# Keeping four engines in written order through the projection of a transformer block, and loading the second half's x later

## Chip, cores and metric

The kernel runs on one core of a Trainium2 chip. The metric is the time of one execution on the device in microseconds (us); the time given for a kernel is the median of several executions.

## What is computed

The reference is one layer of a decoder trunk over 2048 positions of 1024 channels. Cut to what matters here:

```python
h = rms_norm(x, g_mix) * (1.0 + sc1) + sh1      # sh1, sc1 from silu(c) @ w_ada + b_ada
p = h @ w_in                                    # one combined projection, N_IN columns
q_a, k_a, v_a, q_m, k_m, v_m, o_m, u_s, v_s, f_a, i_m, f_m = split(p)
y_attn  = forgetting_attention(rms_norm(q_a), rms_norm(k_a), v_a, f_a)
y_mlstm = sigmoid(o_m) * rms_norm(mlstm_chunkwise(q_m, k_m, v_m, i_m, f_m))
y_sgu   = spatial_gating(gelu(u_s), gelu(v_s), ...)
x = x + gt1 * (concat([y_attn, y_mlstm, y_sgu]) @ w_out)
x = x + gt2 * conv_ffn(rms_norm(x) * (1.0 + sc2) + sh2)
```

Everything that the change touches lies in the first two lines, in the mLSTM and spatial gating groups, and in the start of the attention.

## The kernel before, in words

**The projection.** It takes the first 760 us or so of the execution. The sequence is cut into two halves of 1024 positions, the columns of `w_in` into seven blocks: KM with the gates, QO (queries and output gate of the mLSTM), VM, US (spatial gating), K, Q and V. The 14 steps are the seven blocks for the first half and then QO, KM, VM, US, K, Q and V for the second; "K of the second half" and so on names one of them. A step has eight results, each a tile `acc` in PSUM that 24 matmuls fill: eight parts of the contraction, and for each the three products of a split float32 (`mm3`, L54 to L56, with `wh` and `wl` as the high and low part of the weights and `hh`, `hl` of h).

**The lanes.** The other work is written as generators, called lanes (L459). The function `slot` (L462) is called after each result, and in blocks of 512 columns also after the fourth part of a result, so that half a result is the unit of delay; each call lets every lane that is due write its next piece. Lanes are: the rest of the modulation vectors (`rest_of_mod`), four quarters of the mLSTM (`mlstm(0)` to `mlstm(3)`, with a pace in slots), each closed by `mlstm_end` (L1020: H is divided, squared into `hq` by ScalarE L1032, summed on VectorE L1035, raised to a power on GpSimd L1037, scaled on VectorE L1039, transposed on TensorE L1045, multiplied with the gate `om` and stored in `yt_d`), the spatial gating (`spatial`, L754: two matmuls L761 in one PSUM tile, each read by VectorE L762), the norms and transposes of q and k (`use_qk`, L786: L789, L794, L795, L128, L799, L803, L807, L808, with the stores L810), and `refill`, which loads the eight x tiles of the second half, norms them and transposes them (L589) into h. Before the last step, V of the second half, all lanes are run out in a loop; then the attention's first loads (`kk` L157, `nf` L158, `q` L173, `vv` L163) and its first scores (L206) are written as one more lane beside V's matmuls.

**What sets the order.** Each engine has one queue of instructions. The Python code gives an order, but a scheduler reorders each engine's instructions by its own estimate before the program is built, so what stands in a queue need not be in written order. SyncE (SP) issues the DMAs, in its own queue, one after the other. Tiles of one tag share a number of buffers, and a new tile waits until the oldest has been read for the last time: the tag `t4k` has five buffers (L357) and holds x tiles, `om`, `hq` and the tiles of the spatial gating; raw weights `wr` have three, their split parts `wh` and `wl` eleven each.

**The first block.** KM of the first half is written by `first_block`. It computes part of the modulation on the way (`first_mod`: partial sums on VectorE and GpSimd, then matmuls L447), and norms and transposes the first eight x tiles (L542, L555, L589, L593 to L595).

Of the kernel before, what the change touches and what calls it, by code (L numbers as in the profile page):

```python
# [12 lines left out]
ALU = mybir.AluOpType  # L13
# [20 lines left out]
def trunk(  # L34
# [7 lines left out]
    V, A, G, T = nc.vector, nc.scalar, nc.gpsimd, nc.tensor  # L42
# [84 lines left out]
    def rsqrt(t, n):  # L127
        G.tensor_tensor(t, t, nhalf[:, 0:1].broadcast_to([P, n]) if n > 8 else nhalf[:, :n], op=ALU.pow)  # L128
# [246 lines left out]
    def misc_ps():  # L375
        return pp.tile([P, 512], F32, name="mp", tag="mp")
# [25 lines left out]
    def load_x(tt):  # L402
        xt = pool.tile([P, D], F32, name="xt", tag="t4k")
        dma(xt, x[tt * P : (tt + 1) * P, :])
        return xt
# [53 lines left out]
    def lane(steps_, delay=1, own=False):  # L459
        lanes.append([now[0] + delay, steps_, own])  # L460
# [59 lines left out]
    def small_setup():  # L520
        rows = []
        for i in range(2):
            r = pool.tile([P, P], F32, name="crow", tag="tmpA")
            if i == 0:
                dma(r[0:44], w_conv[0, 0].rearrange("(k p) -> k p", p=P))
                dma(r[44:88], w_conv[0, 1].rearrange("(k p) -> k p", p=P))
            else:
                dma(r[0:44], w_conv[0, 2].rearrange("(k p) -> k p", p=P))
                dma(r[44:88], b_conv[0].rearrange("(k p) -> k p", p=P))
            rows.append(r)  # L530
        yield 3
        for i, r in enumerate(rows):
            ps = misc_ps()
            T.transpose(ps[:, 0:88], r[0:88, :], ident[0:88, 0:88])
            V.tensor_copy(colC[:, i * 88 : (i + 1) * 88], ps[:, 0:88])
            yield 1

    def norm_sums(xt):
        st = pool.tile([P, 2], F32, name="st", tag="st")
        for q in range(2):  # L540
            jk = pool.tile([P, 512], F32, name="jk", tag="sq")
            A.activation(jk, xt[:, q * 512 : q * 512 + 512], AF.Square, accum_out=st[:, q : q + 1])  # L542
        V.tensor_tensor(st[:, 0:1], st[:, 0:1], st[:, 1:2], op=ALU.add)
        st = st[:, 0:1]
        V.tensor_scalar(st, st, 1.0 / D, EPS, op0=ALU.mult, op1=ALU.add)
        rsqrt(st, 1)
        return st
# [37 lines left out]
    def make_h(tb, xs, ks=range(KT)):  # L585
        for k in ks:
            ps = (tr_ps, misc_ps, tr_ps)[k % 3]() if tb == 0 else tr_ps()
            for i in range(4):
                T.transpose(ps[:, i * P : (i + 1) * P], xs[i][:, k * P : (k + 1) * P], ident)  # L589
            h32 = pool.tile([P, TB], F32, name="h32", tag="t2k")  # L590
            hh = pool.tile([P, TB], F32R, name="hh", tag="hT")
            hl = pool.tile([P, TB], F32R, name="hl", tag="hT")
            A.activation(h32, ps, AF.Identity, bias=sh1[:, k : k + 1], scale=a1[:, k : k + 1])  # L593
            V.tensor_copy(hh, h32)
            V.tensor_tensor(hl, h32, hh.bitcast(F32), op=ALU.subtract)  # L595
            hT[tb, k] = (hh, hl)
# [221 lines left out]
    def log_gates():  # L818

        fox, fm = gates[:, :, 64:72], gates[:, :, 32:36]  # L820
        mn = pool.tile([P, 8, 12], F32, name="lg0", tag="lg")
        ab = pool.tile([P, 8, 12], F32, name="lg1", tag="lg")
        for sl, g in ((slice(0, 8), fox), (slice(8, 12), fm)):
            V.tensor_scalar(mn[:, :, sl], g, 0.0, None, op0=ALU.min)
            V.scalar_tensor_tensor(ab[:, :, sl], mn[:, :, sl], 2.0, g, op0=ALU.mult, op1=ALU.subtract)
        A.activation(ab, ab, AF.Exp)
        A.activation(ab, ab, AF.Ln, bias=1.0)
        yield 1
        for sl, g in ((slice(0, 8), fox), (slice(8, 12), fm)):
            V.tensor_tensor(g, mn[:, :, sl], ab[:, :, sl], op=ALU.subtract)  # L830
# [189 lines left out]
    def mlstm_end(t0, H, ecol):  # L1020
# [21 lines left out]
        for j in range(2):  # L1042
# [5 lines left out]
            dma(yt_d[512 + j * P : 640 + j * P, t0 : t0 + 512], yt)  # L1048
            yield 1

    def refill():
        xs = [load_x(8 + t) for t in range(4)]
        yield 3
        for h in range(2):
            pair = xs[2 * h : 2 * h + 2]
            sts = [norm_sums(xt) for xt in pair]
            yield 1
            for xt, st in zip(pair, sts):
                V.tensor_scalar(xt, xt, st, None, op0=ALU.mult)
            yield 1  # L1060
        yield 1
        for k in range(KT):
            make_h(2, xs, (k,))
            if k not in (4, 6):
                yield 1
        xs = [load_x(12 + t) for t in range(4)]
        yield 4
        for h in range(2):
            pair = xs[2 * h : 2 * h + 2]
            sts = [norm_sums(xt) for xt in pair]  # L1070
            yield 1
            for xt, st in zip(pair, sts):
                V.tensor_scalar(xt, xt, st, None, op0=ALU.mult)
        yield 1
        for k in range(0, KT, 2):
            make_h(3, xs, (k, k + 1))
            yield 1
# [60 lines left out]
    def in_turn(*gens):  # L1138
        for g_ in gens:
            yield from g_  # L1140

    for n, (half, i) in enumerate(steps):
        if n == 1:
            lane(in_turn(log_gates(), iter((6,)), small_setup()), 2)
            lane(rest_of_mod(), 1)
        if n == 4:
            lane(in_turn(mlstm(0, 4), mlstm(1, 4)), 2)
        if n == nb - 1:
            lane(refill(), 1)
        if n == nb + 2:  # L1150
            lane(in_turn(log_gates(), iter((2,)), mlstm(2, 2), mlstm(3, 2)), 2)
        if n == len(steps) - 1:
            while any(not ln[2] for ln in lanes):
                slot()
            n_accs[0] = 2
            pool.close("proj_r")
            pp.close("proj_r")
            attention_open_right()

            load_k(0)  # L1160
            first_rows = [], []
            first = [scores(0, tb, load_q(0, tb, "qA"), r) for tb, r in zip((1, 0), first_rows)]
            load_v(0, (0, 1))
            lane(in_turn(*first), 1, True)
        light[0] = i < 3 or (half, i) == (0, 6)
        nxt[0] = Weights(blocks[steps[n + 1][1]][0]) if n + 1 < len(steps) else None
        if n == 0:
            first_block()
        else:
            blocks[i][1](half, cur)  # L1170
        if nxt[0]:
            nxt[0].cast()
        cur = nxt[0]
    pool.close("proj_l")
    pp.close("proj_l")

# [70 lines left out]
    class Block:  # L1247
# [36 lines left out]
        def scale(self, i, fresh=False):  # L1284
            t = pool.tile([P, D], F32, name="x2") if fresh else self.x[i]
            V.tensor_scalar(t, self.x[i], self.st[i][:, 0:1], None, op0=ALU.mult)
            self.xn[i] = t
# [513 lines left out]
```

## Time and profile before

| | us |
|---|---|
| median of three executions | 2659.43 |
| lowest and highest of the three | 2658.65, 2663.71 |
| the profiled execution | 2667.82 |
| its span in the trace | 2666.1 |
| TensorE busy in it | 2572.6 (96%) |
| VectorE, ScalarE, GpSimd busy | 1998.6, 1269.4, 415.5 |

The profiled execution is 8.4 us above the median, and 1.7 us of it lie outside the span of the trace. In the lines of the profile PE is TensorE, DVE VectorE, ACT ScalarE, POOL GpSimd and SP SyncE; L12 is line 12 of the kernel, `out<-in` are the program's tiles without their numbers, and `[4.03 <-DVE hq L1039]` says that the engine sat idle for 4.03 us just before, until VectorE's instruction of line 1039 had written `hq`. A granted clock of 0.5 is TensorE at half speed.

### The profile page before, as it was taken

The numbers are of one execution on the slowest core, as the hardware profiler recorded it, in microseconds if no ns is written. First come the engines' busy times: TensorE is split into PE (matmuls) and PEld (weight loads), VectorE is DVE, ScalarE is ACT, GpSimd is POOL, SyncE is SP. The second block draws the span as 40 slices with busy tenths as digits, with TensorE's granted clock in tenths as the row PEclk, the third lists the DMA queues.
The fourth block names the chain that finished last, engine by engine and source line by source line (L and its number), as shares of the span: only waits on it lengthen the run. The fifth ranks groups of instructions, "written<-read, shape, count | busy, mean of one in ns | idle before, by whom it ended". The sixth has DMA issues, their size and how long they took to land.

```text
span 2666.1 us, 36871 instructions
## 1 busy us (share of the span) xinstructions
PE 2572.6 (96%) x12746; PEld 2129.3 (80%) x12761; DVE 1998.6 (75%) x3460; ACT 1269.4 (48%) x2425; POOL 415.5 (16%) x550
## 2 busy tenths in 40 slices
PE   5999999999989999999989999999999999999999
PEld 5887878988778788777768888888888888888787
DVE  6546565656458888875749888887888887898797
ACT  4322334333258888863445454444444444444443
POOL 5012210123145566630000000000000000000000
PEclk8999989999999999999999999999999999999999
DMA  7525455424554445346742222237222226748533
GB/s 246 175 75 161 139 179 150 127 72 137 144 159 121 123 112 155 111 131 220 261 127 80 88 79 88 79 100 284 90 80 87 80 79 215 260 151 306 181 99 115
DMA packets 297812, 377.52 MB, mean 142 GB/s; under 512 B 31247, under 2 KB 189805, under 8 KB 295577
## 3 DMA queue, kind: packets, MB, share of 16 engines
q1 hardware_dynamic: 297624, 375.16, 44.7%
q8 instruction: 101, 1.65, 0.3%
q14 instruction: 87, 0.70, 0.1%
HBM read 274.34 MB, written 100.74 MB: 141 GB/s over the span
## 4 chain that ended last, share of the span: by engine, by line
PE 76%; DVE 10%; DMA 5%; issue 4%; ACT 3%; POOL 2%; SPq 0%; DVEq 0%; ACTq 0%; POOLq 0%
PE ub L56 10%; PE ub L54 10%; PE ub L55 10%; PE acc L54 5%; PE acc L55 5%; PE acc L56 5%; PE db L55 4%; PE db L56 4%; PE db L54 4%; PE tp L259 3%; PE sp L206 3%; PE op L245 2%; PE op L246 2%; DVE wspl L1545 1%; PE wps L54 1%
## 5 line engine op out<-in xcount | busy, mean ns | idle before, releaser
L54 PE MATMUL acc<-wh,hh 128*128 128x512 f32 (+2 forms) x768 | 287.6, 375 | 1.0 <-ACT wh L624 0.8
L54 PE MATMUL ub<-T,wsph 128*128 128x512 f32 x704 | 274.2, 390 | 5.8 <-ACT wsph L1413 5.8
L55 PE MATMUL acc<-wl,hh 128*128 128x512 f32 (+2 forms) x768 | 275.7, 360 | 0.2 <-DVE wl L625 0.2
L56 PE MATMUL acc<-wh,hl 128*128 128x512 f32 (+2 forms) x768 | 274.8, 360 | 0.0
L56 PE MATMUL ub<-T,wspl 128*128 128x512 f32 x704 | 273.7, 389 | 0.7 <-DVE wspl L1414 0.7
L55 PE MATMUL ub<-T,wsph 128*128 128x512 f32 x704 | 273.9, 389 | 0.0
L55 PE MATMUL db<-wspl,wsph 128*128 128x512 f32 x616 | 240.3, 390 | 1.9 <-DVE wspl L1545 1.9
L56 PE MATMUL db<-wsph,wspl 128*128 128x512 f32 x616 | 239.6, 389 | 0.0
L54 PE MATMUL db<-wsph 128*128 128x512 f32 x616 | 238.2, 389 | 0.3 <-ACT wsph L1544 0.3
L1413 ACT CAST wsph<-S 128x512 fp32r<-128x512 f32 x176 | 109.7, 623 | 227.9 <-PE ub L55 161.7
L263 DVE TENSOR_TENSOR plo<-tp,phi 128x512 fp32r<-128x512 f32 (+1 forms) x320 | 187.0, 607 | 38.1 <-ACT phi L262 35.8
L54 PE MATMUL ub<-B,wsph 128*128 128x512 f32 x528 | 207.1, 392 | 2.8 <-ACT wsph L1413 2.8
L56 PE MATMUL ub<-B,wspl 128*128 128x512 f32 x528 | 206.9, 392 | 0.7 <-DVE wspl L1414 0.7
L55 PE MATMUL ub<-B,wsph 128*128 128x512 f32 x528 | 206.8, 392 | 0.0
L223 ACT ACTIVATE L<-L,nm 128x1024 f32<-128x1024 f32 (+2 forms) x192 | 172.5, 902 | 37.9 <-DVE nm L212 36.6
L262 ACT CAST phi<-tp 128x512 fp32r<-128x512 f32 (+1 forms) x320 | 160.4, 521 | 49.0 <-PE tp L259 46.8
L259 PE MATMUL tp<-ident,L 128*128 128x128 f32 x1088 | 178.1, 275 | 4.7 <-POOL L L228 1.5
L206 PE MATMUL sp<-kk,q 128*128 128x512 f32 (+3 forms) x640 | 169.9, 377 | 7.6 <-DMA q<-q_d 4.4
L228 POOL TENSOR_SCALAR L<-L,rs 128x1024 f32<-128x1024 f32 (+2 forms) x192 | 167.9, 884 | 11.2
L1544 ACT CAST wsph<-act 128x512 fp32r<-128x512 f32 x132 | 82.3, 623 | 178.8 <-PE db L55 157.7
L54 PEld LDWEIGHTS acc<-wh,hh 128*128 128x128 f32 x768 | 147.7, 192 | 20.4 <-ACT wh L624 1.2
L56 PEld LDWEIGHTS acc<-wh,hl 128*128 128x128 f32 x768 | 146.2, 191 | 21.4
(345 smaller groups left out, 6017.1 us busy)
## 6 DMA issues: line engine op xcount, KB each, us to landing
w<-in_w_up_dram SPq DMA_DIRECT2D x88, 512.0 KB
wd<-in_w_down_dram SPq DMA_DIRECT2D x176, 256.0 KB
wa<-in_w_ada_dram SPq DMA_DIRECT2D x96, 256.0 KB
act_d<-yc SPq DMA_DIRECT2D x44, 512.0 KB
act<-act_d SPq DMA_DIRECT2D x44, 512.0 KB
wr<-in_w_in_dram SPq DMA_DIRECT2D x68, 256.0 KB
q<-q_d SPq DMA_DIRECT2D x128, 128.0 KB
hc_d<-hl SPq DMA_DIRECT2D x28, 512.0 KB
```

The lines of the kernel that those rows point to most:

```text
L54: T.matmul(ps, lh, rh, start=start, stop=False, skip_group_check=resume)
L55: T.matmul(ps, lh, rl, start=False, stop=False, skip_group_check=resume)
L56: T.matmul(ps, ll, rh, start=False, stop=stop, skip_group_check=resume)
L206: T.matmul(sp[:, b : b + bw], q2[n][:, qs], kk[:, s0 + b : s0 + b + bw], start=n == 0, stop=n == 1 and not last)
L223: A.activation(L[c], L[c], AF.Exp, bias=nm[:, n - 1 : n], scale=-1.0, accum_out=rs[:, c : c + 1])
L228: G.tensor_scalar(t, t, rs[:, 0:1], 1.0, op0=ALU.mult, op1=ALU.mult)
L245: T.matmul(op[:, c0:], vv[:, j, :], hi[:, c0:], start=(j == 0), stop=False)
L259: T.transpose(tp[:, i * P : (i + 1) * P], rows[i][j // 8][:, (j % 8) * P : (j % 8 + 1) * P], ident)
L262: A.copy(hi[:, c0:], tp[:, c0:])
L263: V.tensor_tensor(lo[:, c0:], tp[:, c0:], hi[:, c0:].bitcast(F32), op=ALU.subtract)
L1413: A.copy(hi, src)
L1544: A.copy(hi, v)
```

## The change

Three edits. A context `manual_schedule` is entered when the second step begins and left after the last one; inside it the queues of TensorE, VectorE, ScalarE and GpSimd keep the written order, while SyncE's queue is still ordered by the scheduler. The lane of `mlstm(0)` gets a pace of 2 slots in place of 4. The lane `refill` starts two slots later, and its norms are written by a new helper, `normed`, in three pieces instead of four.

```diff
+    def normed(xs):
+        scale = lambda pair, sts: [
+            V.tensor_scalar(xt, xt, st, None, op0=ALU.mult) for xt, st in zip(pair, sts)
+        ]
+        first_ = [norm_sums(xt) for xt in xs[:2]]
+        yield 1
+        scale(xs[:2], first_)
+        second_ = [norm_sums(xt) for xt in xs[2:]]
+        yield 1
+        scale(xs[2:], second_)
+        yield 1
+
     def refill():
         xs = [load_x(8 + t) for t in range(4)]
         yield 3
-        for h in range(2):
-            pair = xs[2 * h : 2 * h + 2]
-            sts = [norm_sums(xt) for xt in pair]
-            yield 1
-            for xt, st in zip(pair, sts):
-                V.tensor_scalar(xt, xt, st, None, op0=ALU.mult)
-            yield 1
-        yield 1
+        yield from normed(xs)
...
+    in_order = tc.manual_schedule(
+        engines={mybir.EngineType.PE, mybir.EngineType.DVE, mybir.EngineType.Activation, mybir.EngineType.Pool}
+    )
     for n, (half, i) in enumerate(steps):
         if n == 1:
+            in_order.__enter__()
...
-            lane(in_turn(mlstm(0, 4), mlstm(1, 4)), 2)
+            lane(in_turn(mlstm(0, 2), mlstm(1, 4)), 2)
         if n == nb - 1:
-            lane(refill(), 1)
+            lane(refill(), 3)
...
+    in_order.__exit__(None, None, None)
```

What this does to the queues is seen in three places.

First, TensorE at the end of Q of the second half, before the change. The rows name line, operation, output and inputs; `trp` is the transpose of a normed q, `mps<-ident,hq` the transpose that closes the last quarter of the mLSTM, `acc` with L54 to L56 are V's results, `sp` the attention's first scores.

```order
L803 MATMUL trp<-ident,qn 128x128 x8
L54 MATMUL acc<-wh,hh 128x512
...
L56 MATMUL acc<-wh,hl 128x512
L803 MATMUL trp<-ident,qn 128x128 x4
L54 MATMUL acc<-wh,hh 128x512
...
L1045 MATMUL mps<-ident,hq 128x128 x8
L55 MATMUL acc<-wl,hh 128x512
...
L206 MATMUL sp<-kk,q 128x512 x3
L206 MATMUL sp<-kk,q 128x128 x2
```

The same place after the change:

```order
L803 MATMUL trp<-ident,qn 128x128 x12
L1045 MATMUL mps<-ident,hq 128x128 x8
L54 MATMUL acc<-wh,hh 128x512
L55 MATMUL acc<-wl,hh 128x512
L56 MATMUL acc<-wh,hl 128x512
...
L206 MATMUL sp<-kk,q 128x512 x2
L206 MATMUL sp<-kk,q 128x128 x2
```

Before, 15 of V's matmuls stand ahead of the third transpose of q, 16 more ahead of the transposes of `hq`, and 96 in all (four results) ahead of the first score. Now none stands ahead of the transposes, 12 stand between them and the first score, and from there a score tile follows each dozen of V's matmuls, eight times. SP's queue is the same here but for two stores of V that stood ahead of `kk`: the stores of `yt`, then `kk`, `nf`, `q`, `vv`.

Second, TensorE in K of the first half, at the first tile of the spatial gating (`mp`), before:

```order
L761 MATMUL mp<-sv,wT 128x256
L54 MATMUL acc<-wh,hh 128x512
L55 MATMUL acc<-wl,hh 128x512
L56 MATMUL acc<-wh,hl 128x512
L761 MATMUL mp<-sv,wT 128x256
```

and after the change:

```order
L56 MATMUL acc<-wh,hl 128x512
L761 MATMUL mp<-sv,wT 128x256 x2
L54 MATMUL acc<-wh,hh 128x512
L55 MATMUL acc<-wl,hh 128x512
L56 MATMUL acc<-wh,hl 128x512
```

Three to twelve of the block's matmuls stood between the two halves of such a tile; now none does. There are eight such pairs, four in each half of the sequence.

Third, SP's queue where the x tiles of the second half are loaded, before the change. `wr` are weights, `k_d` the stores of k, `om` the gate that `mlstm_end` of the first quarter multiplies with.

```order
L893 DMA nf_d<-fr 8x512
L404 DMA xt<-in_x_dram 128x1024 x2
...
L404 DMA xt<-in_x_dram 128x1024
L410 DMA wa<-in_w_ada_dram 128x512
L404 DMA xt<-in_x_dram 128x1024
...
L1030 DMA om<-om_d 128x2x512
```

After the change:

```order
L1030 DMA om<-om_d 128x2x512
L810 DMA k_d<-qhi 128x4x128
...
L404 DMA xt<-in_x_dram 128x1024 x2
L810 DMA q_d<-qhi 128x4x128
L404 DMA xt<-in_x_dram 128x1024
...
L1048 DMA yt_d<-yt 128x512
L810 DMA q_d<-qhi 128x4x128
L810 DMA q_d<-qlo 128x4x128
L404 DMA xt<-in_x_dram 128x1024
```

The four x tiles took four of the five `t4k` buffers in K's block, ahead of `om`; now `om` (and `hq` behind it) come first, three x tiles follow in Q's block, and the fourth comes after `hq` has been transposed and stored. In step with this, TensorE's transposes of `hq` stand after half of V's first result instead of near the end of its eighth, and the small matmuls of `mlstm(1)` (L910 to L1001), most of which stood close together behind them among QO's first matmuls of the second half, are spread over V's and QO's results, a piece after each half result.

In the first block, too, which lies ahead of the new context, the order has changed: its first results are written one after the other instead of interleaved, and the norms of x tiles 4 to 7 (L542) stand behind the third result on ScalarE.

More of the change, by code (lines that the diff above doesn't have):

```diff
@@ L1067, in refill @@
         yield 4
[L1068 to L1074, printed above, removed]
+        yield from normed(xs)
         for k in range(0, KT, 2):
```

## The prediction

> **What bounds the kernel now.** The first view is the page. Its line of busy times, with the share of the span and the number of instructions, and the busy time in windows, most of 50 us (time, PE, PEld, DVE, ACT, POOL, then the granted clock, DMA share and GB/s):
>
> ```profile
> PE 2572.6 (96%) x12746; PEld 2129.3 (80%) x12761; DVE 1998.6 (75%) x3460; ACT 1269.4 (48%) x2425; POOL 415.5 (16%) x550
> ```
>
> ```profile
> 0.00:50.00 50.00, 22.28 (x97) 19.52 (x98) 32.51 (x69) 21.58 (x50) 32.67 (x47) 0.90 0.80 273
> 50.00:100.00 50.00, 45.73 (x293) 42.08 (x292) 33.17 (x86) 23.85 (x47) 1.82 (x4) 0.93 0.56 170
> 100.00:150.00 50.00, 50.00 (x302) 44.61 (x302) 17.44 (x34) 8.51 (x15) 0.00 (x0) 1.00 0.54 167
> 200.00:250.00 50.00, 45.04 (x214) 36.58 (x214) 34.30 (x68) 13.72 (x28) 12.77 (x10) 0.97 0.60 181
> 350.00:400.00 50.00, 45.72 (x217) 37.90 (x217) 29.41 (x59) 16.89 (x37) 4.65 (x3) 0.83 0.55 174
> 388.00:398.00 10.00, 9.75 (x46) 8.31 (x45) 2.27 (x6) 3.94 (x12) 0.00 (x0) 0.61 0.49 172
> 700.00:750.00 50.00, 44.02 (x196) 34.90 (x195) 18.47 (x40) 12.69 (x31) 14.71 (x18) 0.97 0.63 176
> ```
>
> TensorE is the bound, and in the projection it is full in most windows (the one from 100 us stands for them); time is to be had only in the first block and at about 220, 380 and 710 us. What ended these waits (engine, line, releaser; us, times, longest), from 86 to 800 us:
>
> ```profile
> PE mps L1045 <- DVE hq L1039: 6.4, 2, 4.0
> PE mp L761 <- DVE sy L762: 5.9, 2, 4.8
> PE sp L206 <- DMA q<-q_d: 4.4, 2, 4.0
> PE trp L803 <- DVE qn L799: 1.8, 1, 1.8
> PE sp L206 <- DVE nm L212: 1.2, 3, 0.7
> ```
>
> So the change can win two stalls, at 380 and at 220 us, with the slow clock behind them; what it can lose is cover, since work of the next block no longer steps into a wait.
>
> **The stall at 380 us: won, -12.0 us.** The timeline of DVE, ACT, POOL and PE, and two rows of the view of the tile `hq` (its columns: shortest, median and longest in ns, and when):
>
> ```profile
> 333.15 1.22 DVE L1028 TENSOR_TENSOR H<-H,den 128x1024 f32<-128x1024 f32 x1
> ```
>
> ```profile
> 372.28 1.05 ACT L1032 ACTIVATE hq<-H 128x1024 f32<-128x1024 f32 x1
> ```
>
> ```profile
> L1035 DVE TENSOR_REDUCE mss<-hq x1: 1214/1214/1214, 375.0 to 375.0; 128x16 f32<-128x1024 f32 x1
> L1039 DVE TENSOR_TENSOR hq<-H,mss x1: 1225/1225/1225, 379.7 to 379.7; 128x1024 f32<-128x1024 f32 x1
> ```
>
> ```profile
> 376.69 3.01 POOL L1037 TENSOR_TENSOR mss<-mss,nhalf 128x16 f32<-128x16 f32 x1 [36.82 <-DVE mss L1036]
> ```
>
> ```profile
> 381.02 1.97 PE L1045 MATMUL mps<-ident,hq 128*128 128x128 f32 x8 [4.03 <-DVE hq L1039]
> ```
>
> H is ready at 334.4, its square is taken at 372.3: for 38 us `hq` has no buffer, as the x tiles hold four of the five. With `hq` allocated first, and its transposes after half of V's first result, square, sum, power and scaling run in Q's block under Q's matmuls. The wait of 4.03 goes. So does the slow clock of 0.83 in this window, 0.17 x 50 = 8.5 us; half a microsecond of it fell into the wait, so 8.0, and 12.0 together. Nearly half of it follows no long wait: from 388 to 398 PE was busy for 9.75 of 10 us at a clock of 0.61, at the crowd of small matmuls of `mlstm(1)`, and these now stand apart between dozens of full ones.
>
> The Trainium skill, "TensorE: Matmul & The Clock Gate", Part 1, ties half speed to an idle window of about 3.4 us and full speed to as long a busy one. By that rule the slow stretch from 388 us, with PE hardly idle, is not explained and need not go: 0.39 x 10 = 3.9 us would stay and the gain be 8.1. I take the row, since the crowd that stood there is gone.
>
> The edits that serve this cost nothing of their own: the pace of 2 only brings H earlier; the x tiles come later, the fourth after `hq` is stored, and their norms (two ACT passes each) lie under V's matmuls while the first of the new L589 stands nine half results into V's block.
>
> **The stall at 220 us: won, -7.4 us; its place taken, +6.5 us.** PE and DVE:
>
> ```profile
> 216.83 0.59 PE L761 MATMUL mp<-sv,wT 128*128 128x256 f32 x2
> ...
> 222.92 1.22 PE L761 MATMUL mp<-sv,wT 128*128 128x256 f32 x2 [4.80 <-DVE sy L762]
> ...
> 224.79 0.63 PE L56 MATMUL acc<-wh,hl 128*128 128x512 f32 x1
> 225.22 0.63 PE L54 MATMUL acc<-wh,hh 128*128 128x512 f32 x1
> ```
>
> ```profile
> 222.44 0.42 DVE L762 TENSOR_TENSOR sy<-mp,gsgu 128x256 f32<-128x256 f32 x1
> ```
>
> The second matmul of a tile waits until DVE has read the first half. DVE was late because the scheduler had put the next quarter's scans ahead of L762; in written order they come later. Both waits (5.9) go, and the slow clock behind them (matmuls every 0.43 us at 224.79 and 225.22; 0.03 x 50 = 1.5 by the window). But each pair now stands together with nothing between, and so waits at every tile: the first matmul to its end 0.59, then from L762's start to PE's next 0.48, less the 0.24 that PE would issue anyway, 0.83. Eight times is 6.6; I take 6.5. Below 4 it cannot well fall (0.48 each); if DVE has a cast of 0.7 in hand each time it is 9. While PE waits the block's matmuls are queued behind.
>
> **The first block: +3 us (-2 to +5).** Rows of DVE, PE (24 matmuls lie between its two) and ACT:
>
> ```profile
> 67.90 0.75 DVE L555 TENSOR_SCALAR xt<-xt,st 128x1024 f32<-128x1024 f32 x1 [0.52 <-POOL st L128]
> ...
> 78.17 0.68 DVE L595 TENSOR_TENSOR hl<-h,hh 128x512 fp32r<-128x512 f32 x1
> ```
>
> ```profile
> 82.00 0.29 PE L54 MATMUL acc<-wh,hh 128*128 128x272 f32 x1
> ...
> 85.00 0.29 PE L54 MATMUL acc<-wh,hh 128*128 128x272 f32 x1
> ```
>
> ```profile
> 60.00 0.63 ACT L542 ACTIVATE jk<-xt 128x512 f32<-128x512 f32 x1 [2.34 <-DMA xt<-in_x_dram]
> ...
> 86.37 0.37 ACT L687 COPY ev<-acc 128x256 f32<-128x256 f32 x1 [1.01 <-issue]
> ```
>
> The norms of the second x tiles began at 60.0, as x landed, and ended at 68.7; h was done at 78.9, and the block's last result was copied from 86.4, 7.5 us after it, since four results are interleaved with the transposes. Now the norms stand behind the third result, but then run one behind the other; I put h 1 us later. All of the last three results' 72 matmuls stand behind it, at 3.00 / 24 = 0.125 each 9.0 us: 79.9 + 9.0 = 88.9, or 2.5 later than 86.4, and 3 with the hand-overs. DVE's casts no longer stand between its sums for the modulation; were all of that to reach h, the block could end 2 us sooner, and with 2 us more in the norms it is +5.
>
> **The end of the projection: +19 us.** PE, the chain of waits, and a window of 5 us:
>
> ```profile
> 698.32 1.03 PE L803 MATMUL trp<-ident,qn 128*128 128x128 f32 x8
> ...
> 711.26 1.97 PE L1045 MATMUL mps<-ident,hq 128*128 128x128 f32 x8 [2.38 <-DVE hq L1039]
> ...
> 718.91 0.39 PE L54 MATMUL acc<-wh,hh 128*128 128x512 f32 x1
> ...
> 724.35 0.39 PE L54 MATMUL acc<-wh,hh 128*128 128x512 f32 x1
> ...
> 728.43 0.63 PE L206 MATMUL sp<-kk,q 128*128 128x512 f32 x2
> 729.41 0.64 PE L206 MATMUL sp<-kk,q 128*128 128x512 f32 x3 [0.35 <-DMA q<-q_d]
> ```
>
> ```profile
> 714.05 2.42 DMA yt_d<-yt
> ...
> 716.92 10.76 DMA q<-q_d
> ...
> 764.03 3.38 DMA q<-q_d
> ```
>
> ```profile
> 720.00:725.00 5.00, 5.00 (x23) 4.14 (x23) 0.43 (x1) 0.37 (x1) 0.00 (x0) 1.00 1.01 285
> ```
>
> Q's matmuls end where the first row stands. From there the chain over H, `hq` and `yt` runs 13 us to L1045, then SP issues `yt`, `kk`, `nf` and `q`, and q lands 10.8 us after its issue, behind kk and nf on DMA engines that are full (1.01). Before, PE did 96 of V's matmuls in that time and lost 1.8 (L803, above) and 2.4 us. Now the chain is the same (the products that close H stand 12 matmuls before Q's end in both orders), but PE has only the 12 transposes of q, the eight of L1045 and 12 matmuls: it is through at about 717 and waits for q until about 729. At full speed, 24 matmuls in 5.44 us (718.91 to 724.35) or 0.227 each, the 84 that it had done more by then are 19.1; with the slow clock behind the wait, 1.5 as at 220 us, and less the waits inside the scores, which V's matmuls now fill (0.35 and 1.2), 19. From below: were q to land as quickly as at 764 (3.38), scores would begin at about 722, when the old kernel was 65 matmuls on, and 53 x 0.227 is 12. From above, with 5 us more in a chain that now stands behind everything written earlier, 24. I take 19, by the row at the same place with the same loads ahead. Nothing gives it back: V's last store still releases the next q, as before.
>
> **Small waits, +2 us (0 to 8).** A new block's last weights are cast in written order, three raw buffers deep; a load of `wr` then lies in the open when it is late. No such wait is in the list above, and in the old order casts ran ahead; the range reaches from nothing to over half a microsecond for each of 13 steps.
>
> The sum: -12.0 - 7.4 + 6.5 + 3 + 19 + 2 = +11.1. The profiled execution would go from 2667.8 to 2678.9; it lay 8.4 above the median of the runs, so for the median 2659.4 + 11.1 = 2670.5.
>
> **Rivals.** *Not slower: the scores start early.* The place is again the end of Q. If DVE reaches L1028 as soon as Q's matmuls end, that row and the four behind it take 1.22 + 1.05 + 1.21 + 3.01 + 1.23 = 7.7 us, L1045 comes at about 706, 5 us sooner; and if q then needs 3.4 us rather than 10.8, it is there at about 717, when the old kernel was some 47 matmuls on: 35 x 0.227 = 7.9, and the sum is 0.0, 2659. No change is what it means as soon as the end costs less than 13 us, faster only below 3. For it: only kk, nf and q are on the queues, no stores of V. Against: the window above is full with just these loads. The Trainium skill, "SBUF — State Buffer", section on the DMA setup-cost knee, gives a transfer a fixed cost of about 2 us and a rate that peaks at 436 GB/s; by an estimate from that page a q tile on idle engines would land within 3 us of its issue. The row of 764 is near that, the one of 717 is not.
>
> *Slower by more: the small waits add up.* In written order an engine that waits holds all behind it: DVE's sums of the modulation (L486) wait for `wa`, and in SP's queue `wa` now stands behind the fourth x tile, which waits for `hq`; the evacuation of V's results stands behind these sums. With 0.9 us for each of 13 steps, 12 in place of 2, the sum is +21: 2680.5.
>
> *The crowd keeps its slow clock.* The gain at 380 us is 8.1 rather than 12.0, the sum +15: 2674.5. (It is what the rule above would have.) For it, PE was not idle there; against, the old order ran the closing matmuls of `mlstm(3)` between full ones (L803 and L54 around 698) with no such loss.
>
> **How the numbers follow.** Forecast 0.45, early scores 0.2, small waits 0.2, slow clock 0.1, something else 0.05. About 0.2% (5.3 us) is what a measurement of this kernel can tell from no change. Early scores split evenly between same and faster; of the forecast a tenth falls within 0.2%; the rest but the unnamed is slower: faster 0.14, same 0.16, slower 0.70. The range takes early scores at their centre and beyond it to 2655 (first block at its low end), and small waits with the upper end of the chain, 2687.
>
> **What would show it.** Right: no wait at L1045 in V of the first half and a clock of 1.00 around 350 to 400 us; eight short waits at L761; the first block's end near 89 us; PE idle for some 12 us ahead of the first L206, with 12 of V's matmuls done. The forecast is wrong if that wait is under 4 us, if the windows between the named places fall below 49 us of PE, or if the chain to L1045 is much longer than 13 us.

## The result, and the profile after

The changed kernel takes 2723.8 us (median of four runs) beside 2661.6 us for the kernel before on the same chip: a ratio of 1.0232, 95% interval 1.0214 to 1.0249. The prediction said slower, by 11 us; it is slower by 62.

First the page's line of busy times, and windows (the columns are those of before): two that were shown of before, from 50 and from 350 us, and four more at places that turned out to matter:

```profile
PE 2591.2 (95%) x12745; PEld 2135.8 (78%) x12761; DVE 2004.6 (74%) x3460; ACT 1264.3 (46%) x2423; POOL 412.6 (15%) x550
```

```profile
50.00:100.00 50.00, 41.73 (x247) 36.38 (x248) 27.94 (x83) 23.16 (x47) 3.50 (x8) 0.87 0.35 111
...
300.00:350.00 50.00, 46.70 (x234) 38.68 (x232) 34.40 (x69) 13.70 (x25) 12.09 (x8) 0.93 0.47 137
350.00:400.00 50.00, 46.43 (x231) 37.87 (x234) 28.68 (x67) 17.09 (x47) 6.14 (x8) 0.90 0.64 198
400.00:450.00 50.00, 43.23 (x220) 34.92 (x221) 29.27 (x66) 21.43 (x48) 3.33 (x5) 0.93 0.55 177
600.00:650.00 50.00, 45.70 (x237) 37.60 (x239) 31.19 (x73) 12.72 (x24) 10.78 (x11) 0.97 0.34 100
...
750.00:800.00 50.00, 35.99 (x147) 28.36 (x148) 14.62 (x31) 9.65 (x24) 12.17 (x14) 0.77 0.48 138
```

The work is the same (the engines' busy times differ by less than 1%), but many windows between the named places are no longer full: from 300 to 450 us PE is busy for 46 or 43 us of 50 and its clock is 0.93 or 0.90. (Not all: the window from 250 us has 49.8 and 1.00.) Before, two of these windows read:

```profile
300.00:350.00 50.00, 50.00 (x262) 42.07 (x263) 32.93 (x77) 18.84 (x45) 9.91 (x8) 1.00 0.52 150
...
400.00:450.00 50.00, 49.92 (x263) 40.43 (x265) 32.17 (x74) 22.21 (x47) 4.12 (x6) 1.00 0.52 157
```

The waits of PE up to 860 us (engine, line, releaser; us, times, longest):

```profile
PE trp L803 <- DVE qn L799: 14.4, 4, 5.9
PE sp L206 <- DMA q<-q_d: 11.5, 3, 8.0
...
PE acc L55 <- DVE wl L625: 8.3, 10, 2.3
PE trp L761 <- DVE sy L762: 6.8, 4, 1.9
PE mp L505 <- DVE modacc L495: 6.1, 1, 6.1
PE mp L761 <- DVE sy L762: 5.8, 4, 1.9
```

The long wait at L1045 of the first half is gone, as forecast. In its place stand many waits, most of them for VectorE, none but the one of 8.0 us for q longer than some six microseconds.

To see where the time went, each step of the projection is measured by its matmuls: a step has 8 x 24 = 192 of them into `acc`, so the time in the trace at which the 192nd, the 384th and so on starts is a mark that all kernels share. The columns give the time between marks, two steps taken together where lanes run across; a prime is the second half of the sequence, and the last column is the last mark. Profiled executions:

```
us                 KM   QO+VM  US+K    Q  V+QO' KM'+VM' US'+K'  Q'   V'    end
before            86.0   68.8  111.1  58.6  132.4   53.5  122.4  65.2  60.3  758.4
after             90.3   72.0  114.0  60.4  145.7   54.0  139.3  65.2  79.2  820.2
difference        +4.3   +3.2   +2.9  +1.8  +13.3   +0.5  +16.9   0.0 +18.9  +61.8
the prediction      +3      -   -4.1     -    -12      -   +3.2     -   +19   +11.1
```

The prediction's row is its terms put to their places: -7.4 and half of the +6.5 in US+K, the other half in US'+K'; its +2 for small waits has no place and is in the sum alone. So the first block and the end of the projection came as forecast. What was missed is 7.0 in US+K, 25.3 in V+QO', 13.7 in US'+K' and 3.5 in the rest after the small waits' 2. (The spans of the two profiled executions differ by 56.6, some 5 us less. What follows the last mark takes between 1901 and 1908 us in the profiled executions of this document, longest in the kernel before, so these 5 us are the variation of single executions. Two executions with the same order in TensorE's queue, the changed kernel and the one with the context entered later, differ by up to 1.4 us in a column.)

### The profile page after: what moved, and what is told of

It is laid out like the page before. It is cut to its first block, busy times and chain, and to the rows that moved or that the text cites. A ratio compares the mean times of both kernels' runs of the same rounds, so it can differ in the third digit from the quotient of the medians.

```text
span 2722.7 us, 36857 instructions
## 1 busy us (share of the span) xinstructions
PE 2591.2 (95%) x12745; PEld 2135.8 (78%) x12761; DVE 2004.6 (74%) x3460; ACT 1264.3 (46%) x2423; POOL 412.6 (15%) x550
## 4 chain that ended last, share of the span: by engine, by line
PE 57%; DVE 6%; DMA 4%; ACT 2%; issue 2%; POOL 1%; SPq 0%; DVEq 0%; ACTq 0%; POOLq 0%
PE ub L54 10%; PE ub L56 10%; PE ub L55 10%; PE db L55 4%; PE db L56 4%; PE db L54 4%; PE sp L206 3%; PE tp L259 3%; PE op L245 2%; PE op L246 2%; DVE wspl L1549 1%; PE wps L54 1%; PE wps L55 1%; PE wps L56 1%; DVE L L212 1%
## 5 line engine op out<-in xcount | busy, mean ns | idle before, releaser
L54 PE MATMUL acc<-wh,hh 128*128 128x512 f32 (+2 forms) x768 | 292.3, 381 | 1.5 <-ACT wh L624 1.0
L55 PE MATMUL acc<-wl,hh 128*128 128x512 f32 (+2 forms) x768 | 281.8, 367 | 11.8 <-DVE wl L625 8.3
L56 PE MATMUL acc<-wh,hl 128*128 128x512 f32 (+2 forms) x768 | 280.8, 366 | 0.6 <-DVE hl L595 0.6
L54 PE MATMUL ub<-T,wsph 128*128 128x512 f32 x704 | 274.4, 390 | 5.8 <-ACT wsph L1417 5.8
L56 PE MATMUL ub<-T,wspl 128*128 128x512 f32 x704 | 273.9, 390 | 0.2 <-DVE wspl L1418 0.2
L56 PE MATMUL db<-wsph,wspl 128*128 128x512 f32 x616 | 239.8, 390 | 0.0
L54 PE MATMUL db<-wsph 128*128 128x512 f32 x616 | 238.4, 390 | 0.3 <-ACT wsph L1548 0.3
L54 PE MATMUL ub<-B,wsph 128*128 128x512 f32 x528 | 208.2, 394 | 2.8 <-ACT wsph L1417 2.8
L56 PE MATMUL ub<-B,wspl 128*128 128x512 f32 x528 | 207.6, 393 | 0.3 <-DVE wspl L1418 0.3
L223 ACT ACTIVATE L<-L,nm 128x1024 f32<-128x1024 f32 (+2 forms) x192 | 172.5, 902 | 32.0 <-DVE nm L212 30.2
L55 PEld LDWEIGHTS acc<-wl,hh 128*128 128x128 f32 x768 | 150.1, 195 | 35.8 <-DVE wl L625 12.3
L56 PEld LDWEIGHTS acc<-wh,hl 128*128 128x128 f32 x768 | 149.6, 195 | 23.9 <-DVE hl L595 1.3
L54 PEld LDWEIGHTS acc<-wh,hh 128*128 128x128 f32 x768 | 150.4, 196 | 22.8 <-ACT wh L624 1.9
```

The costliest lines, as they stand in the source:

```text
L54: T.matmul(ps, lh, rh, start=start, stop=False, skip_group_check=resume)
L55: T.matmul(ps, lh, rl, start=False, stop=False, skip_group_check=resume)
L56: T.matmul(ps, ll, rh, start=False, stop=stop, skip_group_check=resume)
L223: A.activation(L[c], L[c], AF.Exp, bias=nm[:, n - 1 : n], scale=-1.0, accum_out=rs[:, c : c + 1])
```

## The experiments

Each experiment changes the changed kernel, unless its text says otherwise. The theory after the result was that the fault lies in the written order and not in the lanes' new delays, and that it acts at a few places: the two halves of a spatial tile, the casts of weights behind other work, the modulation's last sum, and the end. The rival was that the lanes' own move costs much of it.

**Which half of the change: the lanes alone, and the order of some engines alone.** In the first kernel the context is left out, and only the lanes' delays and the helper `normed` remain:

```diff
-    in_order = tc.manual_schedule(
-        engines={mybir.EngineType.PE, mybir.EngineType.DVE, mybir.EngineType.Activation, mybir.EngineType.Pool}
-    )
-            in_order.__enter__()
-    in_order.__exit__(None, None, None)
```

> The changed kernel without the written order: the pace of 2, the later x tiles and the respaced norms stay, and the scheduler orders all queues as before. Theory (the written order costs the time): within 5 us of the kernel before or faster by up to 12 us, since hq gets its buffer early and the stall of 4.0 us at L1045 and the slow clock behind it can go: 2649 to 2667 us. Rival (the moved lanes themselves cost, because x tiles and norms come late): over 2680 us, with waits at L589 and L505 as in the changed kernel.

2658.9 beside 2663.9: 0.9984 [0.9970, 0.9999]. The theory held: the lanes' move alone costs nothing. The gain at 380 us is there in part: from V to VM' the steps take 127.5 + 50.2 us, 8.2 less than before, and of that 1.8 is lost again in Q.

The next kernels hold fewer engines. First TensorE alone, then the other three without it:

```diff
-        engines={mybir.EngineType.PE, mybir.EngineType.DVE, mybir.EngineType.Activation, mybir.EngineType.Pool}
+        engines={mybir.EngineType.PE}
```

> Written order on TensorE's queue alone; VectorE, ScalarE and GpSimd are ordered by the scheduler. Theory A (TensorE's own order costs: nothing of the next result stands where it could fill a wait): 2705 to 2725 us. Theory B (the order of VectorE and ScalarE costs: casts, sums and norms come late): 2665 to 2685 us, with the waits for wl L625 gone and those of L761 and of the end left.

> Written order on VectorE, ScalarE and GpSimd; TensorE is ordered by the scheduler. Theory A: 2660 to 2680 us, since the scheduler moves matmuls into the waits. Theory B: 2700 us or more, since operands are late whatever TensorE's order.

TensorE alone: 2691.3, 1.0106 [1.0082, 1.0131]. The other three: 2681.8, 1.0073 [1.0044, 1.0101]. Both fell between the theories: neither carries the loss alone. So three more were run, with TensorE and VectorE, VectorE alone, and all but VectorE (the same line, with other engines in the set):

> Written order on TensorE and VectorE. Theory (VectorE's queue is the partner: the second matmul of a pair, L803 and the weights wait for what stands behind scans and casts there): 2715 to 2726 us, as with all four. Rival (ScalarE's order is: its casts wait for raw weights and hold the squares behind them): 2691 to 2703 us.

> Written order on VectorE alone. Theory: about what VectorE, ScalarE and GpSimd cost together, 2678 to 2686 us. Rival (ScalarE's order is what costs): 2658 to 2668 us.

> Written order on TensorE, ScalarE and GpSimd, VectorE by the scheduler. Theory: little more than TensorE alone, 2688 to 2698 us. Rival: 2710 us or more.

2708.5, 1.0176 [1.0143, 1.0209]; 2668.6, 1.0028 [1.0012, 1.0044]; 2695.0, 1.0123 [1.0095, 1.0151]. The second came near its rival's bound and the third as the theory had it; the first lies between. Each median less that of the kernel before on the same chip, and the steps:

```
held in written order    median    US+K  V+QO'  US'+K'   V'
none (lanes alone)         -5.0   111.2  127.5  122.6  59.9
VectorE                    +5.5   107.2  128.2  125.7  67.2
VectorE, ScalarE, GpSimd  +17.9   110.1  130.0  128.8  71.5
TensorE                   +27.4   113.7  128.1  130.9  77.8
TensorE, ScalarE, GpSimd  +31.8   113.6  132.6  127.4  77.0
TensorE, VectorE          +45.4   110.9  138.8  135.1  77.8
all four (the change)     +62.2   114.0  145.7  139.3  79.2
```

Two things are to be read from it. For the end of the projection (V') TensorE's order is enough, 77.8 of the 79.2 us; VectorE's alone lengthens it too (67.2), but adds nothing to TensorE's. And the rest is no sum over engines: ScalarE and GpSimd add 4.4 to TensorE alone, but 12.4 where VectorE is held and 16.8 where both are; V+QO' loses nothing with TensorE or VectorE alone (128.1, 128.2) and 11 us with both. What ScalarE's order adds shows in VectorE's waits for the weights' high part, here of the changed kernel, of the one with TensorE and VectorE, and of the one with VectorE, ScalarE and GpSimd, from 86 to 860 us:

```profile
DVE wl L625 <- ACT wh L624: 93.4, 44, 5.4
```

```profile
DVE wl L625 <- ACT wh L624: 29.7, 21, 3.6
```

```profile
DVE wl L625 <- ACT wh L624: 85.4, 40, 5.4
```

In the kernel before it is 30.2, and between 25.5 and 30.6 in every run that leaves the subtract to VectorE and doesn't hold both ScalarE and VectorE. Only where both are held does VectorE stand idle for some 90 us at L625, with all its later work behind it. (GpSimd is held in each of these runs too; its part was not taken apart.)

The 11 us in V+QO' are another thing, since they are lost with ScalarE free. They begin at one wait; ACT, DVE and PE of the kernel with TensorE and VectorE held:

```profile
409.82 0.62 ACT L624 CAST wh<-wr 128x512 fp32r<-128x512 f32 x1 [4.57 <-DMA wr<-in_w_in_dram]
```

```profile
410.48 0.69 DVE L625 TENSOR_TENSOR wl<-wr,wh 128x512 fp32r<-128x512 f32 x1 [2.79 <-ACT wh L624]
```

```profile
413.91 2.07 PE L505 MATMUL mp<-modacc,ones 128*128 128x512 f32 x2 [6.35 <-DVE modacc L495]
```

Raw weights land late, the cast and the subtract wait for them, and the modulation's sum L495, for which TensorE waits, stands behind the subtract. With VectorE alone held, the same subtract waits 2.57 us, but L505 waits for nothing, as TensorE has other matmuls to do meanwhile; with TensorE alone held, the sum is not behind that subtract, and L505 does not wait either. The experiment that moves these sums (below) takes 11.1 us from V+QO'.

What ScalarE's order does is seen at one tile of the spatial gating, in the timeline of the changed kernel; PE:

```profile
591.54 0.60 PE L761 MATMUL mp<-sv,wT 128*128 128x256 f32 x2
593.99 0.70 PE L761 MATMUL mp<-sv,wT 128*128 128x256 f32 x2 [1.85 <-DVE sy L762]
...
595.72 0.63 PE L55 MATMUL acc<-wl,hh 128*128 128x512 f32 x1
...
598.87 0.59 PE L761 MATMUL trp<-sv,wT 128*128 128x256 f32 x2
601.35 0.70 PE L761 MATMUL trp<-sv,wT 128*128 128x256 f32 x2 [1.88 <-DVE sy L762]
```

ACT at the second of these waits, and DVE at both:

```profile
599.07 0.38 ACT L733 ACTIVATE ev<-acc 128x256 f32<-128x256 f32 x1 [4.22 <-PE acc L56]
599.35 0.38 ACT L734 ACTIVATE su<-acc 128x256 f32<-128x256 f32 x1
599.61 0.62 ACT L624 CAST wh<-wr 128x512 fp32r<-128x512 f32 x1
```

```profile
591.74 1.17 DVE L1010 SCALAR_TENSOR_TENSOR Cst<-Cst,dcol,mps 64x65 f32<-64x65 f32 x4
...
593.51 0.42 DVE L762 TENSOR_TENSOR sy<-mp,gsgu 128x256 f32<-128x256 f32 x1
...
600.26 0.69 DVE L625 TENSOR_TENSOR wl<-wr,wh 128x512 fp32r<-128x512 f32 x1 [3.60 <-ACT wh L624]
600.87 0.42 DVE L762 TENSOR_TENSOR sy<-trp,gsgu 128x256 f32<-128x256 f32 x1
```

It is a ring. ScalarE's next work in written order is to read a result (L733) that TensorE is still computing; the cast L624 stands behind that, though it needs no result and its raw weights were issued before 550 us; VectorE stands at L625 for 3.60 us until the cast is done; L762, for which TensorE waits, stands behind L625. Each engine waits for the one before it, and all three are idle in turn. At the first of the two waits it was updates of the mLSTM's state (L1010) that stood ahead of L762, not a cast. And in sum the waits at L761 do not come from the ring: they are 12.6 us in the changed kernel, but 13.4 with TensorE alone held and 13.2 with all but VectorE. The ring is shown at this place; what it costs in all was not measured by itself.

**The two halves of a spatial tile apart.** The second half goes to another PSUM tile, so that it no longer waits for L762:

```diff
-            if g % 2 == 0:
-                mp = (misc_ps, tr_ps)[g // 2]()
+            mp = (misc_ps, tr_ps)[g % 2]()
```

> The changed kernel with the two spatial gating matmuls of a pair in two different PSUM tiles, so that the second need not wait for VectorE's read of the first. Theory (the pair is a wait of its own): the waits at that line, 12.6 us in all, go, and 3.4 us of slow clock behind the two longest: 2705 to 2713 us. Rival (VectorE is late anyway, and PE meets it a little later): 2718 us or more.

2711.6, 1.0182 [1.0158, 1.0206]: the theory held. Against the changed kernel 12.2 us are gone, 8.2 in US+K and 5.2 in US'+K'; the 12.6 us of L761 in the list of waits are accounted for.

**The low part on GpSimd.** `Weights` lets GpSimd subtract (L625) in place of VectorE, so that nothing stands behind the cast:

```diff
-        nxt[0] = Weights(blocks[steps[n + 1][1]][0]) if n + 1 < len(steps) else None
+        nxt[0] = Weights(blocks[steps[n + 1][1]][0], G) if n + 1 < len(steps) else None
```

> The changed kernel with the low part of the split weights (wl) computed on GpSimd instead of VectorE. Theory (in VectorE's written order the casts stand behind the mLSTM's scans and ahead of norms: so weights are late, their raw buffers come free late, and q's norms wait): the waits for wl, 10.6 us, shrink to a few, the waits at L803 halve, with some slow clock: 2702 to 2712 us. Rival (the raw weights are late since their DMAs are issued and land late, whoever casts): 2717 us or more, with the waits now at the casts of GpSimd or ScalarE.

2720.0, 1.0207 [1.0176, 1.0238]: the rival's time held. US'+K' falls by 10.0, but US+K rises by 2.0, and in the medians only 3.9 are left. TensorE still waits 7.9 us for the low part, now from GpSimd, and 12.9 at L761: taking the subtract, and with it the ring, off VectorE does not cure the pairs.

**The modulation's last sums elsewhere.** A lane adds up the modulation on VectorE in marked steps; its last matmul L505 waited 6.1 us, behind L495 and a cast. The mark is moved from V to Q' (QO', KM' and VM' have it anyway), so that no sum stands there:

```diff
-        light[0] = i < 3 or (half, i) == (0, 6)
+        light[0] = i < 3 or (half, i) == (1, 5)
```

> The changed kernel with the modulation's sums that ran beside V of the first half moved to K of the second half. Theory (VectorE's sums wait there for late wa and hold the row that PE multiplies, 6.1 us at L505 with slow clock behind): 2712 to 2718 us. Rival (the same wait arises at the new place, or VectorE is late there for other reasons): 2721 to 2727 us.

2721.1, 1.0218 [1.0194, 1.0243]: the rival held in the sum. V+QO' falls by 11.1, more than the wait, but 2.4 come back in KM'+VM' and 1.7 in Q'; up to the last mark 4.5 are left, and 2.7 in the medians. (QO+VM, where nothing was changed, took 2.0 more in this execution; the last section has a reason for most of that.)

**The written order left before the last step.**

```diff
         if n == nb - 1:
...
+            in_order.__exit__(None, None, None)
...
-    in_order.__exit__(None, None, None)
```

> The changed kernel with the written order left before the last step, so that the scheduler may again put V's matmuls of the second half among the last transposes. Theory: the last step was 18.9 us longer than before, and all of that comes from the order there: 2703 to 2708 us. Rival (the last step is long because the lanes reach it late, whatever the order in it): over 2716 us.

2708.1, 1.0168 [1.0143, 1.0192]: at the upper bound of the theory. V' takes 64.4 in place of 79.2, still 4.1 more than before, so most of the 18.9 us comes from the order there, not all. In its timeline the transposes of `hq` wait 0.21 us in place of 2.46, and the first scores find their q without the wait of 8.04 that the changed kernel has there (below); PE:

```profile
756.77 1.10 PE L1045 MATMUL mps<-ident,hq 128*128 128x128 f32 x8 [0.21 <-DVE hq L1039]
...
774.08 1.02 PE L206 MATMUL sp<-kk,q 128*128 128x512 f32 x5
```

**All of these together, with the subtract on GpSimd and on VectorE.** The first kernel has the edits of the four experiments above; the second, run last, has all but that of `Weights`.

> The three edits together, and the written order left before the last step. Theory (the 60 us are these four mechanisms, and nothing else is left): 2658 to 2672 us, about the kernel before. Rival (the written order costs at every place, and a cured wait shows at the next): 2680 us or more.

> Written order left ahead of the last projection step, the two L761 products of a pair in separate accumulators, the late casts' sums moved off the spot ahead of L505, and the low-half subtract kept on VectorE. Theory (the rest that e9 kept over the kernel before came from the subtract on GpSimd, 1.36 us for 0.70): 2660 to 2669 beside a kernel before of about 2663. Rival (the written order itself keeps the rest, whichever engine subtracts): 2674 or more.

2676.8, 1.0062 [1.0041, 1.0084], between theory and rival; and 2692.0, 1.0103 [1.0055, 1.0151], the rival. With the end, the pair and the sums set right, and VectorE's subtract, the kernel is still some 30 us slower than the one before. Of the 15 us between the two, 12.2 are in US'+K' (136.3 and 124.1). There PE's longest wait with VectorE's subtract, and the queue of DVE that made it:

```profile
530.47 0.80 PE L55 MATMUL acc<-wl,hh 128*128 128x512 f32 x1 [3.67 <-DVE wl L625]
```

```profile
526.94 0.68 DVE L495 TENSOR_TENSOR modacc<-modacc,brow 1x512 f32<-1x512 f32 x1
527.63 0.68 DVE L894 TENSOR_TENSOR ra<-ra,rb 4x512 f32<-4x512 f32 x1
...
529.28 0.42 DVE L898 TENSOR_SCALAR R<-ra 4x512 f32<-4x512 f32 x1
529.73 0.69 DVE L625 TENSOR_TENSOR wl<-wr,wh 128x512 fp32r<-128x512 f32 x1
```

(Past L759 this program's numbers are one lower.) The weights' low part, for which a matmul waits, stands behind pieces of the modulation and of the mLSTM's scans that were written earlier. The expectation that GpSimd's subtract was what kept the 15 us fell: in written order it gains some 15. The 15.2 us that are left with all four edits were not divided further.

**The same on the free order.** Two kernels without the context: the pair apart alone, and with the subtract on GpSimd as well.

> No written order: the moved lanes, and the spatial gating matmuls of a pair in two PSUM tiles. Theory (the wait of 5.3 us at that line in the run with the moved lanes alone is a wait for VectorE's read, and nothing takes its place): 2650 to 2656 us, 0.2 to 0.5% under the kernel before. Rival (VectorE is late for the next reader as well): 2656 to 2661 us.

> The same with the low part of the weights computed on GpSimd. Theory (under the scheduler the casts are hidden anyway): within 4 us of the run without it. Rival (VectorE's work for the casts delays the chain ahead of the last step, which grows shorter without it): faster by 5 us or more.

2649.7, 0.9944 [0.9930, 0.9958], at the low end of the theory; and 2672.1, 1.0033 [1.0020, 1.0046], which neither theory had. The first beats both kernels, by 0.56% the one before. The window at which the old stall stood, and the first of PE's waits from 86 to 860 us (past L759 this program too is one line shorter, so L1044 is L1045):

```profile
350.00:400.00 50.00, 49.84 (x277) 41.55 (x277) 31.56 (x71) 19.89 (x44) 1.23 (x2) 1.00 0.69 220
```

```profile
PE mps L1044 <- DVE hq L1038: 4.4, 2, 2.3
PE sp L206 <- DMA q<-q_d: 3.1, 1, 3.1
```

So the lanes' move with the pair apart has most of what the change was forecast to win at 380 us (from V to VM' 7.8 us of the 12.0), and the order's price falls away. In the second, GpSimd's subtract costs 22 us; its own group, and that of VectorE in the changed kernel:

```profile
L625 POOL TENSOR_TENSOR wl<-wr,wh 128x512 fp32r<-128x512 f32 x80 | 106.1, 1344 | 89.7 <-ACT wh L624 87.5 <-PE acc L55 1.1 <-PE mp L511 1.1
```

```profile
L625 DVE TENSOR_TENSOR wl<-wr,wh 128x512 fp32r<-128x512 f32 x80 | 54.7, 696 | 72.5 <-ACT wh L624 71.9 <-issue 0.3
```

It takes 1.34 us for 0.70. The same edit that gains 3.9 us in the changed kernel, and some 15 with the three others, costs 22 where VectorE may choose its order.

**The context entered later**, with the fourth step (`n == 3`) in place of the second, in the changed kernel and in the one with all four edits:

```diff
+        if n == 3:
+            in_order.__enter__()
         if n == 1:
-            in_order.__enter__()
```

> The changed kernel with the written order entered at the fourth step instead of the second. Theory (a start of the written order fences the steps ahead of it, so that the first block's results cannot be interleaved, and QO's casts come late: the first two steps took 148.7 instead of 141.9 us): 2714 to 2718 us. Rival (the first two steps are slow for reasons of the lanes, or the loss moves on): 2721 us or more.

> The kernel with the three edits and the end free, and the written order entered at the fourth step. Theory (what is left of its 15 us lies mostly in the first two steps): 2667 to 2672 us. Rival (it is spread over the written steps): 2674 us or more.

2723.6, 1.0219 [1.0202, 1.0236], and 2679.3, 1.0057 [1.0042, 1.0072]: the rival in both. The first block still takes 90.5 us and QO+VM 72.0. So the start of the written order is not why the first block is longer.

## Why the prediction was wrong, point by point

**The small waits: the step that failed.** "Small waits, +2 us (0 to 8)" was argued from the list of waits of before, in whose lines shown no cast stands (further down the same list TensorE waits once for one, 0.8 us at L54). That list is of a schedule in which the casts had been moved ahead of their need; it could not show what they cost when they may not. In the changed kernel PE's own waits for L625 are 10.6 us (8.3, and 2.3 at L56, below), and 6.1 more at L505, where the subtract stands ahead of the sum. In US'+K' the subtract in VectorE's queue is worth 10.0 us by the experiment that moves it, 12.2 with the other edits in. And with the end, the pairs and the sums set right, the kernel is still 31.7 us slower, where the prediction's terms without the end and the pairs come to -14.4. The rival "the small waits add up" had the mechanism, the sums of the modulation and the evacuation included, but at 0.9 us a step, and it looked to a late `wa` where at L505 raw weights were late; the steps from QO to Q' lost 38.6 us (+61.8 less the first block and V'), where the prediction's terms for them, the 2 of small waits included, came to -10.9.

```profile
98.16 0.50 PE L56 MATMUL acc<-hh,wl 128*128 128x512 f32 x1 [2.28 <-DVE wl L625]
```

**The stall at 380 us: the wait went, the gain didn't come.** "The wait of 4.03 goes. So does the slow clock": the L1045 wait fell to 1.29 (and is for `dcol`, no longer for `hq`), but the windows from 300 to 450 us have 0.93, 0.90 and 0.93, that is 12.0 us of slow clock for the 8.5 of before, and two new waits stand around it; PE:

```profile
340.33 1.09 PE L803 MATMUL trp<-ident,qn 128*128 128x128 f32 x4 [3.23 <-DVE qn L799]
353.55 1.11 PE L1045 MATMUL mps<-ident,hq 128*128 128x128 f32 x4 [1.29 <-ACT dcol L920]
...
424.56 2.07 PE L505 MATMUL mp<-modacc,ones 128*128 128x512 f32 x2 [6.10 <-DVE modacc L495]
```

Waits of 10.6 us and 12.0 of clock against 4.0 and 8.5 are about 10 of the +13.3 here; with the smaller waits in, PE is idle for 14.2 us of these two steps against 4.4, which with the clock is all of it. The moved lanes do rid TensorE of most of the slow clock, as the prediction said, as long as TensorE and VectorE are not both held: in the lanes alone this stretch is 4.9 shorter. The rival that the crowd keeps its slow clock had 3.9 us of it stay; 12.0 are there, and that they are the crowd's is not shown: the slow stretches here, from 339, 353, 387 and 421 us, each lie beside a new wait (3.23, 1.29, 0.99 and 6.10 us), with small matmuls near some of them.

**The stall at 220 us and the pairs.** That each of the eight pairs would wait was right, and the wait of 4.8 us is gone. The price was not right: 12.6 us for the eight, 1.6 each in place of 0.83, since L762 does not start when the matmul ends but stands behind other work of VectorE, at the two places shown a state update and a cast. The upper bound of 9 allowed for one cast of 0.7 in hand; it left out that VectorE may be waiting itself. By the experiment the pairs cost 8.2 us in US+K and 5.2 in US'+K', slow clock behind the waits included, where the forecast had about 3.2 in each: that is 5 of the 7.0 missed in US+K, but only 2 of the 13.7 in US'+K', where the subtract weighs more (above).

**The first block, +3: measured +4.3**, inside its range; its matmuls end at 90.6. Its last result was copied later than the 89 forecast, at 94.0, since on ScalarE a cast that waits for raw weights stands ahead of the copy (before, the copy at 86.37 stood ahead of such a cast):

```profile
93.51 0.62 ACT L624 CAST wh<-wr 128x512 fp32r<-128x512 f32 x1 [3.84 <-DMA wr<-in_w_in_dram]
94.04 0.37 ACT L687 COPY ev<-acc 128x256 f32<-128x256 f32 x1
```

What makes the block longer was only argued. It is not the context's start; it is longer with more engines held (86.5 with none, 88.0 with TensorE, 90.3 with all, but 91.3 without VectorE), and stays open.

**The end of the projection, +19: measured +18.9**, by the chain as told in the main. PE, from the end of Q':

```profile
741.19 0.60 PE L803 MATMUL trp<-ident,qn 128*128 128x128 f32 x4
746.16 1.09 PE L803 MATMUL trp<-ident,qn 128*128 128x128 f32 x4 [4.38 <-DVE qn L799]
753.19 1.09 PE L803 MATMUL trp<-ident,qn 128*128 128x128 f32 x4 [5.94 <-DVE qn L799]
756.75 1.97 PE L1045 MATMUL mps<-ident,hq 128*128 128x128 f32 x8 [2.46 <-DVE hq L1039]
771.27 0.76 PE L206 MATMUL sp<-kk,q 128*128 128x512 f32 x1 [8.04 <-DMA q<-q_d]
```

The transposes of `hq` come 15.6 us after the first row (13 were forecast) and the scores 30.1 (30.7 by the rows of before, 698.3 to 729). PE is idle for 8.0 us ahead of the scores rather than some 12, because it has waited 10.3 between the transposes of q. The long waits also leave TensorE at half speed for longer than the 1.5 us taken: the window from 750 us has 0.77, and PE is busy for 58.1 us of V' where it was 54.3, so that up to 3.7 of the 18.9 may be this. That the sum came out so exactly is in part luck. The rival of early scores needed q in 3.4 us; it was waited for.

## What to carry to other kernels

A list of waits is a list for one order: what it does not show may be what the order was made to hide. Before an order is fixed, look, on each engine, for work that has an early input and a waiting reader (here the casts of weights) and see what would stand ahead of it; and count the engines that are held together, since two queues in a fixed order can stop each other where either alone does not. When a change has two parts, a placing of work and a fixing of its order, time them apart: here the first was worth 0.16%, and 0.56% with one more edit, while the second cost 2.5%.

## What was not expected of the hardware

TensorE fell to half speed behind single waits of about two microseconds, but not every time. Around 600 us (columns as above):

```profile
595.00:600.00 5.00, 4.46 (x13) 3.20 (x11) 1.56 (x5) 0.93 (x3) 0.61 (x1) 0.66 0.00 0
...
602.00:606.00 4.00, 4.00 (x13) 3.09 (x11) 2.79 (x6) 1.51 (x3) 1.59 (x2) 0.58 0.23 63
```

The matmuls shown above at 593.99 and 601.35 waited 1.85 and 1.88 us; from 595.3 and from 602.0 the next ones come every 0.43 us instead of 0.23, each time for about 3.4 us. But behind the wait of 2.28 us at 98.16 (above) matmuls come every 0.23 us, while in the kernel with the pairs apart the same wait, 2.29 us, ends at half speed:

```profile
98.50:102.00 3.50, 3.06 (x7) 2.48 (x8) 2.06 (x7) 2.18 (x4) 0.00 (x0) 0.51 0.75 240
```

So the length of such a wait alone does not decide it, and QO+VM differs by some 1.7 us (half of 3.4) between executions for this. The Trainium skill, "TensorE: Matmul & The Clock Gate", Part 1, gives idle and busy windows of about 3.4 us between half and full speed. The length of the slow stretches agrees; that an idle window as long must come first does not, as here 1.9 us were enough.
